# Distance penalty moved into a per-head mask tile, and the 64-row second pass paired on two row halves

## The chip, the cores and the metric

The kernel runs on one core of a Trainium2 chip. The metric is the time of one execution on the device in microseconds; three runs of the kernel before the change are given. The profile is one further, profiled execution of the same program.

## The reference

One layer of a decoder block on 512 tokens of width 1024: RMSNorm, one wide input projection, two token mixers side by side (gated linear attention, GLA, and sparse attention, NSA), a merge, an output projection, and a SwiGLU feed-forward part. The change touches NSA alone. It has 8 heads of width 64 in 2 groups, and three branches; the selected branch ("s") and the window branch ("w") both come to a causal attention over 512 keys, each with its own keys and values, because 8 blocks of 64 keys exist and up to 16 are selected, and the window is 512 wide. What both compute:

```
slopes = exp2(-8 * (h + 1) / 8)                     # 2^-(h+1), h = 0..7
s = q @ k.T - slopes * (t - pos)                    # distance penalty
s = where(pos <= t, s, -1e30)
p = softmax(s);  o = p @ v
out = gate0 * o_compressed + gate1 * o_selected + gate2 * o_window
```

## The kernel before

**Numbers.** All data is four-byte. A product is split into high and low parts (`whi`, `wlo`; `hT_hi`, `hT_lo`), and three matmuls (hi·hi, lo·hi, hi·lo; lines 182 to 184) make one k-step of a dense product.

**The stages** run in this order: token-wise projections, GLA beside further projections, compression for NSA, the attention loop, the merge and output projection, the feed-forward part. The program is written for a scheduler: the order in the code, with the readiness of data, sets the order on each engine; pools of buffers with a fixed number of turns (`bufs`) set when a buffer comes free. PSUM banks are taken by tag, two to a tag: `sc` for scores, `tp` for transposes, `acc` for a head's output, `mm` for dense products.

**The attention loop** (`attention`, line 846) runs over 16 units: head h = 0 to 7, and for each head the branches s and w. In a unit it turns the probabilities of this unit by TensorE transposes (L792), splits them into `ph` (ScalarE, L199) and `pl` (VectorE, L200), and multiplies them with the values (L806, L807, L809). Between these it does the scores of the unit two ahead, and fills gaps with single k-steps of dense products (`fill`, lines 182 to 184), eight k-steps a unit, which is one dense product. The weights of these are converted by ScalarE (L59 `whi`, L62 `wlo`) and finished by an accumulating DMA that GpSimd issues (L63 `wlo`), one in most units.

**Scores** (`scores`, line 727). The 512 queries are four blocks of 128; block i needs 128 (i + 1) keys, so its products have 128, 256, 384 or 512 columns. A unit's four blocks go in three parts: block 3 in one PSUM bank; blocks 0 and 2 in another; block 1 in a third turn. The first pass (L742) multiplies `q1`, which holds the high part of the query on one half of the 128 rows and its low part on the other, with `ka`, which holds the high part of the keys on both halves. The second pass (L743) multiplies `q3`, the high query on rows 0 to 63 and two more rows, with `kb`, the low part of the keys on rows 0 to 63 and two more rows. The two extra rows (64 and 65, from `augq` and `augk`) carry the distance penalty: -slope · t times 1, and slope times pos. Hence 66 rows. VectorE then adds the causal mask, negates and takes the row's extreme in one operation (L750, `causal` is 128 x 512 with zeros and a triangle of -1e30 at its right end), and ScalarE exponentiates (L752).

`head_setup` (line 710) makes `q1` and `q3` of a head, once per head, two heads ahead; `group_keys` (line 696) makes `ka` and `kb` once per group and branch.

**Elsewhere, for reference:** L632 and L638 are two small products of the compression, on rows 0 to 63 and on rows 64 to 127; L183 behind L638 is a part of a dense product.

Of the kernel before, what the change touches and what calls it, by code (L numbers as in the profile page):

```python
# [8 lines left out]
F32 = mybir.dt.float32  # L9
F32R = mybir.dt.float32r  # L10
U8 = mybir.dt.uint8
AF = mybir.ActivationFunctionType
OP = mybir.AluOpType
# [3 lines left out]
S = 512  # L17
# [8 lines left out]
NEG = -1e30  # L26
# [66 lines left out]
def hybrid_block_kernel(ctx: ExitStack, tc: tile.TileContext, I, outT):  # L93
    nc = tc.nc
    act, dve, pool, pe = nc.scalar, nc.vector, nc.gpsimd, nc.tensor
# [5 lines left out]
    def bank(tag):  # L101
        return psum.tile([128, 512], F32, tag=tag, bufs=2, name="ps_" + tag)
# [52 lines left out]
    for key in with_gla + with_cmp + with_att + late:  # L155
        kind, n = key
# [45 lines left out]
    def token_sums(acc, tag, blocks=range(NT)):  # L202

        ps = bank(tag)
        for a in range(len(acc)):
            for i in blocks:
                pe.matmul(ps[:, i:i + 1], acc[a][:, i * 128:(i + 1) * 128], ones[:, 0:1],
                          start=(a == 0 and i == blocks[0]), stop=(a == len(acc) - 1), skip_group_check=True)
        return ps
# [6 lines left out]
    def over_partitions(rs, tag, blocks=range(NT), after=None):  # L216
        ps = bank(tag)
        with tc.issue_after(after.ins) if after else nullcontext():
            for i in blocks:
                pe.matmul(ps[:, i * 128:(i + 1) * 128], rs[:, i:i + 1].to_broadcast([128, 128]), ident,  # L220
                          start=True, stop=True)
        return ps
# [6 lines left out]
    for k in range(KD):  # L229
        xt = xin.tile([128, S], F32, tag="xt", bufs=8, name="xt")  # L230
        nc.sync.dma_start(xt, I["xT"][k])
        if k % 2 == 0:
            st.ahead_to(min(k // 2 + 1, 2))
        last = act.activation(out=hT[:, k, :], in_=xt, func=AF.Copy, scale=g_pre[:, k:k + 1])
        dve.scalar_tensor_tensor(out=hTl[:, k, :], in0=xt, scalar=g_pre[:, k:k + 1],
                                 in1=hT[:, k, :].bitcast(F32), op0=OP.mult, op1=OP.subtract)
# [12 lines left out]
    for g in range(3):  # L249
        pss = [bank(t) for t in tags[g]]  # L250
        for c in range(4):
            wh, wl = st.next(("tok", g, c))
            for i in range(NT):
                if (g, c, i) == (0, 3, 2):
                    ps = token_sums([acc_x], "acc")
                    rsqrt_mean(rs_x, ps[:, 0:NT], D, EPS)
                t = slice(i * 128, (i + 1) * 128)
                for kk in range(2):
                    k = 2 * c + kk
                    w = slice(kk * TG, (kk + 1) * TG)  # L260
                    o = pss[i][:, 0:TG]
# [3 lines left out]
        if g == 0:  # L265
            ps = over_partitions(rs_x, "acc")
            act.copy(rb_x, ps)
            p_in.__exit__(None, None, None)
            mid = p_mid.__enter__()
# [5 lines left out]
        for i in range(NT):  # L275
            c0, c1 = g * TG, (g + 1) * TG
            if c0 < 1024:
                act.activation(out=tok[i][:, c0:min(c1, 1024)], in_=pss[i][:, 0:min(c1, 1024) - c0], func=AF.Copy,
                               scale=rs_x[:, i:i + 1])
            if c1 > 1024:  # L280
                act.activation(out=tokb[:, i, 0:c1 - 1024], in_=pss[i][:, 1024 - c0:TG], func=AF.Copy,
                               scale=rs_x[:, i:i + 1])
    C_VS, C_VW, C_GATE, C_A = 0, 128, 256, 280

    causal = mid.tile([128, S], F32, name="causal")
    pool.memset(causal, 0.0)
    pool.dma_start(causal[:, S - 128:S], I["tril_neg"])
    qst = [mid.tile([128, S], F32, tag="qst%d" % i, name="qst%d" % i) for i in range(4)]
    kst = {b: mid.tile([128, S], F32, name="kst" + b) for b in "sw"}
    gq = [base.tile([128, S], F32, tag="b%d" % h, name="gq%d" % h) for h in range(HG)]  # L290
# [26 lines left out]
    for i in range(2):  # L317
        t = gt.tile([128, NT, 128], F32, name="at%d" % i)
# [233 lines left out]
    mid2 = p_mid2.__enter__()  # L552
    p_nsa = tc.tile_pool(name="nsa", bufs=1, reuse_waits="tile")
    nsa = p_nsa.__enter__()
    augq = nsa.tile([66, S], F32, name="augq")
    pool.dma_start(augq[64:66], I["aug"][:, 0, :])
    gates = nsa.tile([128, NT, 24], F32, name="gates")
    act.activation(out=gates, in_=tokb[:, :, C_GATE:C_GATE + 24], func=AF.Tanh, scale=0.5)
    dve.tensor_scalar(out=gates, in0=gates, scalar1=0.5, scalar2=0.5, op0=OP.mult, op1=OP.add)
# [9 lines left out]
    p_sco = tc.tile_pool(name="sco", bufs=1, reuse_waits="tile", side="right")  # L569
    cmp = p_cmp.__enter__()  # L570
    cin = p_cin.__enter__()
    augk = cin.tile([66, S], F32, name="augk")
    pool.dma_start(augk[64:66], I["aug"][:, 1, :])
    cmp_bias = cmp.tile([128, NT, HN, 32], F32, name="cmp_bias")
    pool.dma_start(cmp_bias, I["cmp_bias"])
    cmp_mask = cmp.tile([128, NT, 32], F32, name="cmp_mask")
# [112 lines left out]
    ka, kb, vv = {}, {}, {}  # L689
    for b in "sw":  # L690
        kb[b] = nsa.tile([128, S], F32R, name="kb" + b)
        ka[b] = nsa.tile([128, S], F32R, name="ka" + b)
        vv[b] = nsa.tile([128, NT, 128], F32R, name="vv" + b)
        pool.tensor_copy(kb[b][64:66, :], augk[64:66, :])

    def group_keys(g, b):
        a, o = slice(g * 64, g * 64 + 64), slice((1 - g) * 64, (1 - g) * 64 + 64)
        act.copy(ka[b][a, :], kst[b][a, :])
        dve.tensor_copy(ka[b][o, :], kst[b][a, :])
        dve.tensor_tensor(out=kb[b][0:64, :], in0=kst[b][a, :], in1=ka[b][a, :].bitcast(F32), op=OP.subtract)  # L700

    def group_values(g, b):
        c = (C_VS if b == "s" else C_VW) + g * 64
# [4 lines left out]
    heads = {}  # L708

    def head_setup(h):  # L710
        e = h % 2
        q = qst[h // 2]
        a, o = slice(e * 64, e * 64 + 64), slice((1 - e) * 64, (1 - e) * 64 + 64)
        q1 = nsa.tile([128, S], F32R, tag="q1", bufs=2, name="q1")
        q3 = nsa.tile([66, S], F32R, tag="q3", bufs=2, name="q3")
        act.copy(q1[a, :], q[a, :])
        dve.tensor_tensor(out=q1[o, :], in0=q[a, :], in1=q1[a, :].bitcast(F32), op=OP.subtract)
        act.copy(q3[0:64, :], q[a, :])
        dve.tensor_scalar(out=q3[64:66, :], in0=augq[64:66, :], scalar1=2.0 ** -(h + 1), scalar2=None,
                           op0=OP.mult)  # L720
        heads[h] = (q1, q3)

    OFF = [0, 128, 384, 768]
    sco = []
# [1 line left out]

    def scores(h, b):

        q1, q3 = heads[h]
        p = sco[0].tile([128, 1280], F32, tag="p", bufs=3, name="p")  # L730
        mx = sco[0].tile([128, NT], F32, tag="mx", bufs=3, name="mx")
        z = sco[0].tile([128, NT], F32, tag="z", bufs=3, name="z")
        units[h, b] = p

        def part(blks, last):
            ps = bank("sc")
            col = 0
            for i in blks:
                n = 128 * (i + 1)
                s = ps[:, col:col + n]  # L740
                t = slice(i * 128, (i + 1) * 128)
                pe.matmul(s, q1[:, t], ka[b][:, 0:n], start=True, stop=False)  # L742
                pe.matmul(s, q3[0:66, t], kb[b][0:66, 0:n], start=False, stop=True)  # L743
                col += n
            col = 0
            for i in blks:
                n = 128 * (i + 1)
                s = ps[:, col:col + n]
                o = p[:, OFF[i]:OFF[i] + n]
                dve.tensor_tensor_reduce(out=o, in0=s, in1=causal[:, S - n:S], scale=-1.0, scalar=-NEG,  # L750
                                         op0=OP.add, op1=OP.min, accum_out=mx[:, i:i + 1])
                act.activation(out=o, in_=o, func=AF.Exp, scale=-1.0, bias=mx[:, i:i + 1],  # L752
                               accum_out=z[:, i:i + 1])
                col += n
            if last:
                dve.reciprocal(z, z)
                dve.tensor_tensor(out=z, in0=z, in1=gates[:, :, 3 * h + (1 if b == "s" else 2)], op=OP.mult)
                for i in range(NT):
                    n = 128 * (i + 1)
                    o = p[:, OFF[i]:OFF[i] + n]  # L760
                    dve.tensor_scalar(out=o, in0=o, scalar1=z[:, i:i + 1], scalar2=None, op0=OP.mult)

        return [lambda: part((3,), False), lambda: part((0, 2), False), lambda: part((1,), True)]

    accs = {}

# [60 lines left out]
    def begin(u):  # L827
        h, b = u
        if h % 4 == 0:
            group_keys(h // 4, b)  # L830
        return scores(h, b)

    def first_scores():

        parts = []

        def start():
            p_cin.__exit__(None, None, None)
            sco.append(p_sco.__enter__())
            head_setup(0)  # L840
            for u in order_u[:2]:
                parts.extend(begin(u))

        return [start] + [lambda i=i: parts[i]() for i in range(6)] + [lambda: head_setup(1)]

    def attention(fill):

        head_compressed(0)
        for i, (h, b) in enumerate(order_u):
            nxt = begin(order_u[i + 2]) if i + 2 < len(order_u) else [lambda: None] * 3  # L850
            if b == "s":
                head_start(h)
            elif h + 2 < HN:
                head_setup(h + 2)
# [34 lines left out]
    q = Pieces(with_att)  # L889
# [8 lines left out]
    for n in range(8):  # L898
        ps = bank("sc")
# [60 lines left out]
    for n in range(3):  # L960
        ps = bank("mm")
# [120 lines left out]
    made = {}  # L1082
# [199 lines left out]
    first = (bank("sc"), bank("sc"))  # L1282
# [23 lines left out]
    third = (bank("acc"), bank("acc"))  # L1306
# [22 lines left out]
    for n in range(N0, KF):  # L1329
# [3 lines left out]
        last = unit(n, rest_of_forms if n == N0 else None)  # L1333
# [98 lines left out]
    for n in range(8):  # L1432
        ps = bank("acc" if n % 2 == 0 else "tp")
# [195 lines left out]
```

## Time and profile before

| | |
|---|---|
| time, median of 3 runs | 872.35 us (871.92 to 873.64) |
| profiled execution, span of its instructions | 870.5 us, 13817 instructions |
| profiled execution, its own time | not recorded beside its span; the runs' median lies 1.9 us above the span |
| TensorE busy | 856.8 us (98%), 5268 matmuls |
| TensorE weight loads | 759.8 us (87%) |
| VectorE, ScalarE, GpSimd busy | 594.5 (68%), 486.3 (56%), 141.5 us (16%) |

How to read it: PE is TensorE's matmuls, PEld its weight loads (shown apart, since a load runs under the matmul before it), DVE is VectorE, ACT ScalarE, POOL GpSimd. L742 is line 742 of the kernel. A matmul's shown duration contains its way through the array, so a row of matmuls overlaps; the distance from one start to the next is what it costs. Form 64\*128 means 64 rows and 128 columns of the array in use.

### The profile page before, as it was taken

What the parts mean: (1) busy time and instruction counts of PE and PEld (TensorE: products, weight loads), DVE (VectorE), ACT (ScalarE), POOL (GpSimd) and SP (SyncE); (2) the same over time, 40 slices, a digit from 0 to 9 for tenths busy, and PEclk for the clock granted to TensorE, in tenths of its full rate; (3) what the DMA queues carried; (4) which work ended last, traced back from release to release, by engine and by line L of the source; (5) the groups of instructions that cost most, each with busy time, mean ns of one, the idle gap of its engine ahead of it and who ended that gap; (6) DMA issues with size and microseconds to landing.
All of it is one profiled execution on the core that took longest, in us unless ns stands there. A gap on an engine that the chain in (4) does not pass through costs nothing.

```text
span 870.5 us, 13817 instructions
## 1 busy us (share of the span) xinstructions
PE 856.8 (98%) x5268; PEld 759.8 (87%) x5268; DVE 594.5 (68%) x1125; ACT 486.3 (56%) x862; POOL 141.5 (16%) x169
## 2 busy tenths in 40 slices
PE   9999999999999999999999999999999999999995
PEld 8998877887888788888887999899999999889995
DVE  8224753534464888887767468998778779829876
ACT  7335434333362788888744577765666656525441
POOL 1000322020030001000000354111111110001343
PEclk9999999999999999999999999999999999999998
DMA  7332221222241444545317849679877873335222
GB/s 237 97 98 93 97 83 63 79 66 74 73 152 49 120 98 103 117 98 122 85 49 226 269 137 247 125 199 233 186 171 176 195 176 85 94 87 170 86 98 98
DMA packets 36914, 111.23 MB, mean 128 GB/s; under 512 B 4236, under 2 KB 6300, under 8 KB 36720
## 3 DMA queue, kind: packets, MB, share of 16 engines
q1 hardware_dynamic: 27232, 82.49, 29.7%
q0 software_dynamic: 8896, 27.32, 16.8%
q8 instruction: 41, 0.67, 0.3%
q10 hardware_dynamic: 720, 0.54, 0.2%
q14 instruction: 25, 0.20, 0.1%
HBM read 95.66 MB, written 4.19 MB: 115 GB/s over the span
## 4 chain that ended last, share of the span: by engine, by line
PE 91%; ACT 4%; DVE 2%; issue 1%; DMA 1%; POOL 0%; SPq 0%; ACTq 0%; DVEq 0%; POOLq 0%
PE ps_mm L182 11%; PE ps_mm L184 11%; PE ps_mm L183 11%; PE ps_mm L1191 6%; PE ps_tp L1191 6%; PE ps_sc L1191 5%; PE ps_acc L1191 5%; PE ps_sc L1482 4%; PE ps_acc L1482 2%; PE ps_mm L1482 2%; PE ps_tp L792 2%; PE ps_acc L184 1%; PE ps_acc L183 1%; PE ps_acc L182 1%; PE ps_sc L182 1%; PE ps_sc L184 1%
## 5 line engine op out<-in xcount | busy, mean ns | idle before, releaser
L59 ACT CAST whi<-wraw 128x1024 fp32r<-128x1024 f32 (+2 forms) x81 | 80.1, 989 | 150.4 <-PE ps_mm L183 66.9
L182 PE MATMUL ps_mm<-hT_hi,whi 128*128 128x512 f32 x344 | 139.9, 407 | 0.0
L184 PE MATMUL ps_mm<-hT_hi,wlo 128*128 128x512 f32 x344 | 137.0, 398 | 0.0
L183 PE MATMUL ps_mm<-hT_lo,whi 128*128 128x512 f32 x344 | 136.1, 395 | 0.0
L65 DVE TENSOR_TENSOR wlo<-wraw,whi 128x1024 fp32r<-128x1024 f32 (+2 forms) x66 | 75.0, 1137 | 51.1 <-ACT whi L59 51.0
L184 PEld LDWEIGHTS ps_mm<-hT_hi,wlo 128*128 128x128 f32 x344 | 64.7, 188 | 15.4 <-DVE wlo L65 0.3
L182 PEld LDWEIGHTS ps_mm<-hT_hi,whi 128*128 128x128 f32 x344 | 64.9, 189 | 14.0
L183 PEld LDWEIGHTS ps_mm<-hT_lo,whi 128*128 128x128 f32 x344 | 64.9, 189 | 13.0
L752 ACT ACTIVATE p<-p,mx 128x512 f32<-128x512 f32 (+1 forms) x64 | 35.9, 561 | 8.8 <-DVE mx L750 7.8
L200 DVE TENSOR_TENSOR pl<-ps_tp,ph 128x512 fp32r<-128x512 f32 (+1 forms) x64 | 31.0, 489 | 13.2 <-ACT ph L199 12.5
L63 POOL DMA_DIRECT2D wlo<-wraw x15 | 13.0, 864 | 154.2 <-ACT wlo L62 154.2
L750 DVE CUSTOM_DVE_ANT_0 p<-ps_sc,causal 128x512 f32<-128x512 f32 (+1 forms) x64 | 30.2, 486 | 6.2 <-PE ps_sc L743 6.1
L1090 POOL DMA_DIRECT2D w_uu<-in_w_up x19 | 16.4, 865 | 84.6 <-PE ps_sc L1191 27.0
L199 ACT CAST ph<-ps_tp 128x512 fp32r<-128x512 f32 (+1 forms) x64 | 26.3, 415 | 4.1 <-PE ps_tp L792 3.6
L792 PE MATMUL ps_tp<-ident,p 128*128 128x128 f32 x160 | 27.7, 273 | 0.4 <-ACT pc L686 0.3
L792 PEld LDWEIGHTS ps_tp<-ident,p 128*128 128x128 f32 x160 | 20.6, 140 | 8.0 <-ACT pc L686 0.7
L182 PE MATMUL ps_mm<-gla_hi,whi 128*128 128x512 f32 x64 | 26.2, 410 | 0.0
L466 DVE TENSOR_TENSOR sr<-ps_mm,rb_x 128x512 f32<-128x512 f32 x8 | 5.5, 692 | 29.0 <-PE ps_mm L184 29.0
L184 PE MATMUL ps_mm<-gla_hi,wlo 128*128 128x512 f32 x64 | 25.3, 395 | 0.0
L183 PE MATMUL ps_mm<-gla_lo,whi 128*128 128x512 f32 x64 | 25.3, 395 | 0.0
L1106 ACT CAST w_hl<-s 128x1024 fp32r<-128x1024 f32 x12 | 12.6, 1047 | 19.6 <-issue 15.8
L1106 ACT CAST w_d1h<-s 128x1024 fp32r<-128x1024 f32 x13 | 13.7, 1051 | 17.2 <-issue 12.5
(862 smaller groups left out, 2778.2 us busy)
## 6 DMA issues: line engine op xcount, KB each, us to landing
wraw<-in_w_t SPq DMA_DIRECT2D x40, 512.0 KB, 3.5
wraw<-in_w_gate SPq DMA_DIRECT2D x21, 512.0 KB, 5.8
rw<-in_w_up SPq DMA_DIRECT2D x19, 512.0 KB, 4.2
wlo<-wraw POOLq DMA_DIRECT2D x15, 512.0 KB, 4.5
wlo<-in_w_gate POOLq DMA_DIRECT2D x13, 512.0 KB, 7.2
wraw<-in_w_tok SPq DMA_DIRECT2D x12, 440.0 KB, 4.1
w_uu<-in_w_up POOLq DMA_DIRECT2D x19, 256.0 KB, 5.8
wraw<-in_w_proj SPq DMA_DIRECT2D x8, 512.0 KB, 3.5
```

The source lines that it names most:

```text
L59: self.nc.scalar.copy(hi[:, :cols], raw[:, :cols])
L65: self.nc.vector.tensor_tensor(out=lo[:, :cols], in0=raw[:, :cols], in1=hi[:, :cols].bitcast(F32), op=OP.subtract)
L182: pe.matmul(ps[:, t], wh[:, c], xh(k)[:, t], start=(k == 0), stop=False)
L183: pe.matmul(ps[:, t], wh[:, c], xl(k)[:, t], start=False, stop=False)
L184: marks.append(pe.matmul(ps[:, t], wl[:, c], xh(k)[:, t], start=False, stop=(k == ktot - 1)))
L199: act.copy(hi, src)
L200: dve.tensor_tensor(out=lo, in0=src, in1=hi.bitcast(F32), op=OP.subtract)
L750: dve.tensor_tensor_reduce(out=o, in0=s, in1=causal[:, S - n:S], scale=-1.0, scalar=-NEG, op0=OP.add, op1=OP.min, accum_out=mx[:, i:i + 1])
L752: act.activation(out=o, in_=o, func=AF.Exp, scale=-1.0, bias=mx[:, i:i + 1], accum_out=z[:, i:i + 1])
L792: pe.transpose(tp[:, i * 128:(i + 1) * 128], p[:, OFF[i] + k * 128:OFF[i] + (k + 1) * 128], ident)
L1191: pe.matmul(o, w[:, c], x[q], start=(first and q == 0 and i == 0), stop=(q == 3 and i == 2), skip_group_check=True)
L1482: pe.matmul(o, w[:, c], x[q], start=(first and q == 0 and i == 0), stop=(q == KH - 1 and i == 2), skip_group_check=True)
```

## The change

A tile of 128 x 512 per head takes the place of `causal`: it holds the distance penalty and the causal mask together, and VectorE's operation reads it instead (L760 after). Two such tiles take turns (`alibi`). GpSimd makes them: a DMA broadcasts the positions, a second one adds the triangle, the first operation adds -t per row and halves, and each later head's tile is half of the one before. The mask value is halved with it and stays far below every score. The two extra rows, `augq`, `augk` and their copies go, and the second pass has 64 rows.

```diff
-    causal = mid.tile([128, S], F32, name="causal")
-    pool.memset(causal, 0.0)
-    pool.dma_start(causal[:, S - 128:S], I["tril_neg"])
+    alibi = [mid.tile([128, S], F32, name="alibi%d" % i) for i in range(2)]
+    pool.dma_start(alibi[0], I["aug"][1, 1, :].partition_broadcast(128))
+    pool.dma_start(alibi[0][:, S - 128:S], I["tril_neg"], accum_op=OP.add)
+    alibi_row = mid.tile([128, 1], F32, name="alibi_row")
+    pool.dma_start(alibi_row, I["aug"][0, 0, S - 128:S].unsqueeze(1))
...
-    augq = nsa.tile([66, S], F32, name="augq")
-    pool.dma_start(augq[64:66], I["aug"][:, 0, :])
...
-        pool.tensor_copy(kb[b][64:66, :], augk[64:66, :])
...
-        dve.tensor_tensor(out=kb[b][0:64, :], in0=kst[b][a, :], in1=ka[b][a, :].bitcast(F32), op=OP.subtract)
+        for r in (a, o):
+            dve.tensor_tensor(out=kb[b][r, :], in0=kst[b][a, :], in1=ka[b][a, :].bitcast(F32), op=OP.subtract)
...
-        q3 = nsa.tile([66, S], F32R, tag="q3", bufs=2, name="q3")
+        q2 = nsa.tile([128, S], F32R, tag="q2", bufs=2, name="q2")
+        cb = alibi[(h + 1) % 2]
...
-        act.copy(q3[0:64, :], q[a, :])
-        dve.tensor_scalar(out=q3[64:66, :], in0=augq[64:66, :], scalar1=2.0 ** -(h + 1), scalar2=None,
-                           op0=OP.mult)
-        heads[h] = (q1, q3)
+        act.copy(q2[o, :], q[a, :])
+        if h == 0:
+            pool.tensor_scalar(out=cb, in0=alibi[0], scalar1=alibi_row, scalar2=0.5, op0=OP.add, op1=OP.mult)
+        else:
+            pool.tensor_scalar(out=cb, in0=alibi[h % 2], scalar1=0.5, scalar2=None, op0=OP.mult)
+        heads[h] = (q1, (q1, q2) if e == 0 else (q2, q1), cb)
...
+        def products(groups):
+            banks = [bank("sc") for _ in groups]
+            for ps, blks in zip(banks, groups):
+                for i, n, c in cols(blks):
+                    pe.matmul(ps[:, c], q1[:, i * 128:(i + 1) * 128], ka[b][:, 0:n], start=(i == blks[0]),
+                              stop=False, skip_group_check=True)
+            for e, (ps, blks) in enumerate(zip(banks, groups)):
+                for i, n, c in cols(blks):
+                    pe.matmul(ps[:, c], his[e][half[e], i * 128:(i + 1) * 128], kb[b][half[e], 0:n],
+                              start=False, stop=True, skip_group_check=True)
+            return banks
...
+        def first():
+            made.extend(products(((3,), (0, 2))))
+            softmax(made[0], (3,), False)
+
+        def third():
+            softmax(products(((1,),))[0], (1,), True)
+
+        return [first, lambda: softmax(made[1], (0, 2), False), third]
```

The high query now stands on both row halves, in `q1` on one and in `q2` on the other, and the low keys on both halves of `kb`. Block 3's second pass runs on rows 0 to 63 and those of blocks 0 and 2 on rows 64 to 127, into another bank; block 1's runs on rows 0 to 63 alone. The matmuls are as many as before.

On TensorE, a unit's scores stood in two places, with two k-steps and transposes between them (`ps_sc` are scores, `ps_tp` transposes, `ps_mm` dense products). Before:

```order
L792 MATMUL ps_tp<-ident,p 128x128 x4
L742 MATMUL ps_sc<-kaw,q_2308 128x512
L743 MATMUL ps_sc<-kbw,q_2309 128x512
L182 MATMUL ps_mm<-gla_hi,whi 128x512
L183 MATMUL ps_mm<-gla_lo,whi 128x512
L184 MATMUL ps_mm<-gla_hi,wlo 128x512
L182 MATMUL ps_mm<-gla_hi,whi 128x512
L183 MATMUL ps_mm<-gla_lo,whi 128x512
L184 MATMUL ps_mm<-gla_hi,wlo 128x512
L792 MATMUL ps_tp<-ident,p 128x128 x3
L742 MATMUL ps_sc<-kaw,q_2308 128x128
L743 MATMUL ps_sc<-kbw,q_2309 128x128
```

The same unit after (L748 is the first pass, L752 the second, L810 the transposes; `q_2307` is `q1`, `q_2308` is `q2`):

```order
L810 MATMUL ps_tp<-ident,p 128x128 x4
L748 MATMUL ps_sc<-kaw,q_2307 128x512
L748 MATMUL ps_sc<-kaw,q_2307 128x128
L748 MATMUL ps_sc<-kaw,q_2307 128x384
L752 MATMUL ps_sc<-kbw,q_2308 128x512
L752 MATMUL ps_sc<-kbw,q_2307 128x128
L752 MATMUL ps_sc<-kbw,q_2307 128x384
L182 MATMUL ps_mm<-gla_hi,whi 128x512
L183 MATMUL ps_mm<-gla_lo,whi 128x512
L184 MATMUL ps_mm<-gla_hi,wlo 128x512
```

First and second passes of blocks 3, 0 and 2 now stand together ahead of the two k-steps, the three first passes first; the part of blocks 0 and 2 moved up by two k-steps and the second transposes. Block 1's part stays behind the third transposes.

On GpSimd, the pieces around the start of the attention loop (`wlo` are the accumulating DMAs of the dense weights). Before:

```order
L694 CAST kbs<-augk 2x512
L694 CAST kbw<-augk 2x512
L594 COPY ct<-cpe 128x16 x2
L63 DMA wlo<-wraw 128x1024 x15
L955 TENSOR_TENSOR acc_4264<-acc_4264,nsq 128x512 x2
```

After:

```order
L592 COPY ct<-cpe 128x16 x2
L63 DMA wlo<-wraw 128x1024
L721 TENSOR_SCALAR alibi_574<-alibi_573 128x512
L63 DMA wlo<-wraw 128x1024 x2
L721 TENSOR_SCALAR alibi_573<-alibi_574 128x512
L63 DMA wlo<-wraw 128x1024 x2
```

The two casts are gone, and six halvings stand among the fifteen issues, one per head from head 2 on. The tiles of heads 0 and 1 are made early, behind the DMAs of `alibi`, ahead of GLA's first work on GpSimd.

On VectorE, the same unit as above for TensorE (`pl` is the remainder of transposed probabilities, the ISA rows are the mask operation and its row extreme `mx`). Before:

```order
L750 ISA p,mx<-ps_sc,causal 128x512
L750 ISA mx 128x1
L200 TENSOR_TENSOR pl<-ps_tp,ph 128x512
L200 TENSOR_TENSOR pl<-ps_tp,ph 128x384
L750 ISA p,mx<-ps_sc,causal 128x128
L750 ISA mx 128x1
L750 ISA p,mx<-ps_sc,causal 128x384
```

After:

```order
L760 ISA p,mx<-ps_sc,alibi_573 128x512
L760 ISA mx 128x1
L200 TENSOR_TENSOR pl<-ps_tp,ph 128x512
L760 ISA p,mx<-ps_sc,alibi_573 128x128
L760 ISA mx 128x1
L760 ISA p,mx<-ps_sc,alibi_573 128x384
L760 ISA mx 128x1
L200 TENSOR_TENSOR pl<-ps_tp,ph 128x384
```

The operations on blocks 0 and 2 moved ahead of the second transposes' remainder.

More of the change, by code (lines that the diff above doesn't have):

```diff
@@ L571, in hybrid_block_kernel @@
     cin = p_cin.__enter__()
-    augk = cin.tile([66, S], F32, name="augk")
-    pool.dma_start(augk[64:66], I["aug"][:, 1, :])
     cmp_bias = cmp.tile([128, NT, HN, 32], F32, name="cmp_bias")
@@ L727, in scores @@
     def scores(h, b):
-        q1, q3 = heads[h]
+        q1, his, cb = heads[h]
         p = sco[0].tile([128, 1280], F32, tag="p", bufs=3, name="p")
@@ L733, in scores, with cols, softmax @@
         units[h, b] = p
-        def part(blks, last):
-            ps = bank("sc")
-            col = 0
+        half = (slice(0, 64), slice(64, 128))
+        def cols(blks):
+            at, col = [], 0
             for i in blks:
[L739 to L748, printed above, removed]
+                at.append((i, 128 * (i + 1), slice(col, col + 128 * (i + 1))))
+                col += 128 * (i + 1)
+            return at
+        def products(groups):
[9 more added lines that the diff above has]
+            return banks
+        def softmax(ps, blks, last):
+            for i, n, c in cols(blks):
+                s = ps[:, c]
                 o = p[:, OFF[i]:OFF[i] + n]
-                dve.tensor_tensor_reduce(out=o, in0=s, in1=causal[:, S - n:S], scale=-1.0, scalar=-NEG,
+                dve.tensor_tensor_reduce(out=o, in0=s, in1=cb[:, S - n:S], scale=-1.0, scalar=-NEG,
                                          op0=OP.add, op1=OP.min, accum_out=mx[:, i:i + 1])
@@ L753, in part @@
                                accum_out=z[:, i:i + 1])
-                col += n
             if last:
@@ L761, in part @@
                     dve.tensor_scalar(out=o, in0=o, scalar1=z[:, i:i + 1], scalar2=None, op0=OP.mult)
-        return [lambda: part((3,), False), lambda: part((0, 2), False), lambda: part((1,), True)]
+        made = []
+        def first():
[4 more added lines that the diff above has]
+        return [first, lambda: softmax(made[1], (0, 2), False), third]
     accs = {}
```

## The prediction

> **What bounds the kernel now.** I read the page's span, its busy line and its chain first, then the attention stage alone, because every line that the change touches works there or feeds it.
>
> ```profile
> span 870.5 us, 13817 instructions
> PE 856.8 (98%) x5268; PEld 759.8 (87%) x5268; DVE 594.5 (68%) x1125; ACT 486.3 (56%) x862; POOL 141.5 (16%) x169
> PE 91%; ACT 4%; DVE 2%; issue 1%; DMA 1%; POOL 0%; SPq 0%; ACTq 0%; DVEq 0%; POOLq 0%
> 298.00:438.00 140.00, 139.32 (x752) 113.97 (x750) 113.27 (x326) 116.18 (x259) 11.16 (x13) 1.00 0.45 105
> ```
>
> The last row is the attention loop, from its first transposes to its end: us, then busy PE, PEld, DVE, ACT and POOL, then the granted clock (1.00). TensorE is never idle for long, VectorE and ScalarE are busy 81% and 83% of the time. The waits of the same stretch say whether TensorE waits for them:
>
> ```profile
> POOL wlo L63 <- ACT wlo L62: 114.1, 13, 11.4
> ...
> PEld ps_acc L807 <- DVE pl L200: 2.3, 6, 0.5
> ...
> PEld ps_tp L792 <- ACT pc L686: 0.7, 1, 0.7
> PEld ps_tp L792 <- DVE pl L200: 0.6, 1, 0.6
> ```
>
> Columns: total us, times, longest. TensorE's weight loads wait under 4 us in 140, and part of that lies under a running matmul. So a microsecond added to TensorE's own work here is a microsecond of the end, and one taken away is gained until ScalarE, 17% behind, ends last. The chain of waits gives the price of each matmul as the distance to the next. One unit (a head and a branch; there are 16):
>
> ```profile
> 326.12 0.44 PE ps_tp L792 x4
> 326.56 0.23 PE ps_sc L742
> 326.79 0.23 PE ps_sc L743
> ...
> 328.74 0.06 PE ps_sc L742
> 328.80 0.11 PE ps_sc L743
> 328.92 0.22 PE ps_sc L742
> 329.14 0.18 PE ps_sc L743
> ...
> 330.69 0.12 PE ps_sc L742
> 330.81 0.12 PE ps_sc L743
> ...
> 335.56 0.44 PE ps_tp L792 x4
> ```
>
> A unit is 335.56 - 326.12 = 9.4 us. The L742 and L743 rows are block 3 (512 columns), blocks 0 and 2 (128 and 384), block 1 (256). A second pass (L743) costs 0.23 + 0.11 + 0.18 + 0.12 = 0.64 us a unit, 10.2 us in all. From 256 to 512 columns is 0.11 us, so 0.43 ns a column: 512 columns stream in 0.22 us, and about 0.01 is lost between matmuls. The 128 columns cost 0.11, not 0.06, and the weight loads say why:
>
> ```profile
> 328.58 0.19 PEld L743 LDWEIGHTS ps_sc<-kbw,q 66*128 66x128 f32 x1
> 328.69 0.19 PEld L742 LDWEIGHTS ps_sc<-kaw,q 128*128 128x128 f32 x1
> 328.81 0.19 PEld L743 LDWEIGHTS ps_sc<-kbw,q 66*128 66x128 f32 x1
> ```
>
> A load occupies its path for 0.11 us, with 66 rows as with 128, and normally lies under the matmul before it.
>
> **The change, part by part.**
>
> *The pair.* Block 3's second pass (0.23) now stands beside those of blocks 0 and 2 (0.11 + 0.18), on the other 64 rows: 0.52 us a unit is at stake. Nothing in the trace runs two matmuls at once. Bounds: no overlap, gain 0; whole overlap, 0.23 remains and the gain is 0.29. Three loads are still needed, and the rows show them one after the other: with block 0's load at the start of block 3's matmul, the other half ends 0.11 + 0.11 + 0.16 (384 columns) = 0.38 later, 0.39 with the gap. I take that, since its 0.11 is a row: 0.13 gained a unit, 2.1 us in 16. Block 1's pass has no partner and gains nothing.
>
> *The switches.* Before, 66 rows use the whole array; now 64 rows use half, so each unit goes from the whole array to halves and back twice (pair, block 1): 4 x 16 = 64 switches. Nearly no row of before shows one, but the compression does: L638 multiplies on rows 64 to 127, and the next instruction is a whole-array matmul (L183), which waits for no semaphore.
>
> ```profile
> 273.78 0.19 PEld L638 LDWEIGHTS ps_sc<-cw,chid 64*64 64x64 f32 x2
> 274.03 0.19 PEld L183 LDWEIGHTS ps_mm<-hT_lo,whi 128*128 128x128 f32 x1
> 274.14 0.19 PEld L184 LDWEIGHTS ps_mm<-hT_hi,wlo 128*128 128x128 f32 x1
> ```
> ```profile
> 273.78 0.32 PE L638 MATMUL ps_sc<-cw,chid 64*64 64x64 f32 x2
> 274.04 0.50 PE L183 MATMUL ps_mm<-hT_lo,whi 128*128 128x512 f32 x1
> ```
> ```profile
> L638 PE MATMUL ps_sc<-cw,chid x2: 218/242/267, 273.8 to 273.9; 64*64 64x64 f32 x2
> ```
>
> L638's second matmul takes 0.22, so it started at 273.78 + 0.32 - 0.22 = 273.88. The next load should start then; it starts 0.15 later. 64 columns stream in 0.03, so 0.12 us pass until the array is empty, and then the load itself is uncovered (the load behind it, L184's, starts another 0.11 later, when L183's own matmul can start). That this is no matter of columns or of a narrow matmul is shown by L807, which uses 64 columns and all rows:
>
> ```profile
> 332.73 0.28 PE L807 MATMUL ps_acc<-pl,vvw 128*64 128x256 f32 x1
> ```
> ```profile
> 332.73 0.19 PEld L182 LDWEIGHTS ps_mm<-gla_hi,whi 128*128 128x128 f32 x1
> ```
>
> There the whole-array load starts with the matmul, at 332.73: no wait. So a switch of rows costs 0.12 (emptying) + 0.11 (uncovered load) - about 0.02 of gaps = 0.21 us behind a matmul of 256 or more columns. Bounds: 0 (if L638 is a special case) and 0.23. At L638 itself, where 0.11 of load was the pace anyway, it was 0.14. I take 0.21, because that is what these rows give for long matmuls: 64 x 0.21 = 13.4 us.
>
> The Trainium skill, "TensorEngine Tiling (Array Packing)", Key Properties, says that changing the tiling mode, not just the tile, drains TensorE. The L638 rows agree (0.12 us), the L807 rows show no such drain for a change of columns alone; by the page each of the 64 switches drains, and its sum is the one above.
>
> *VectorE and ScalarE.* The rows of augq go, and each group's key remainder is written on both halves:
>
> ```profile
> L719 DVE TENSOR_SCALAR q<-augq 2x512 fp32r<-2x512 f32 x8 | 3.3, 418 | 0.2
> L700 DVE TENSOR_TENSOR kbs<-ksts,kas 64x512 fp32r<-64x512 f32 x2 | 1.7, 872 | 0.1
> L700 DVE TENSOR_TENSOR kbw<-kstw,kaw 64x512 fp32r<-64x512 f32 x2 | 1.4, 684 | 0.0
> ```
>
> Minus 8 x 0.42 = 3.3, plus 4 x 0.69 to 0.87 = 3.1: nothing, and TensorE covers it. The mask operand of the reduction keeps its shape; ScalarE's second copy only changes its rows. VectorE now gets three reductions together ahead of the remainder of the second transposes; it has 19% to spare, and if it has not, L807 waits, at most 0.5 us at a time as above.
>
> *GpSimd.* At the start one memset and one DMA become three DMAs and two operations, each behind the last one's landing. They stand where GpSimd has nothing to do:
>
> ```profile
> 25.77 0.60 POOL L287 DMA_DIRECT2D causal<-in_tril_neg  x1
> 95.05 0.73 POOL L391 TENSOR_TENSOR gke<-gk,e 128x256 f32<-128x256 f32 x1 [68.68 <-ACT el L375]
> ```
> ```profile
> DMA to landing us min/median/max: 2.2/2.2/2.2
> ```
>
> The last row is L287's DMA. 68 us cover three such landings and two operations, some 10 us. Two DMAs of augq and augk and two casts go. Six halvings of 128x512 stand among the issues of wlo; each has a unit (9.4 us) before its head needs it. Bounds for one: a memset of that shape and a two-operand sum.
>
> ```profile
> L319 POOL MEMSET at<- 128x512 f32 x2 | 1.1, 549 | 0.0
> L1503 POOL TENSOR_TENSOR acc<-acc,nsq 128x512 f32<-128x512 f32 x3 | 6.8, 2272 | 20.8 <-ACT nsq L1502 10.8 <-ACT acc L1499 10.0
> ```
>
> 0.55 to 2.3 us; I take 1.1 (one operand, nearer the memset). The 114 us in which GpSimd waits for ScalarE cover six of them. They wait for reductions that ended over a unit earlier, so the DMAs behind them are not held up. Cost nothing.
>
> **Sum.** 13.4 - 2.1 = 11.3 us more for TensorE. A later TensorE waits less for VectorE: of the listed waits I let 1 us vanish. So +10.3: a span of 870.5 + 10.3 = 880.8 us. The runs' median, 872.35, lies 1.9 above the profiled span; added to it, 882.7. I say 882.
>
> **The rivals.**
> 1. *Both kinds of switch cost, as summed* (0.48). With a pair that overlaps wholly and switches at 0.14 it is 9.0 - 4.6 - 1 = +3.4; with no overlap and nothing absorbed +13.4. So 875.8 to 885.8 at its ends, mostly 878 to 885.
> 2. *Only the way back costs* (0.16): the half-array load may slip under a running whole-array matmul; L638 shows a way back only. 32 x 0.21 - 2.1 - 0.5 = +4.1: 876.5.
> 3. *Switches are free and the pair overlaps* (0.26), the case on the other side. Place: the second pass of blocks 0, 2 and 3. Price: 16 x 0.13 to 0.29 = 2.1 to 4.6 us gained, 867.8 to 870.3. For it speaks that L638 is one event, a four-byte product with an own wait ahead of it; against it that L183 waits for nothing else. It decides where a switch costs under 0.13 / 4 = 0.03 us (0.07 with whole overlap).
> 4. *No overlap and no switch cost* (0.10): the change does not do what it says, the halves run one after the other: within 1 us, 872.4.
>
> The Trainium skill, "TensorE: Matmul & The Clock Gate", Part 3, says that matmuls on different row groups run at once, a few ns apart. By it the pair costs 0.23; no run here shows it; with free switches that is rival 3's lower end, 867.8.
>
> **How the numbers follow.** About 0.2% (1.7 us) is what a measurement of this kernel can tell from no change. Rivals 1 and 2 are slower (0.64), 4 is the same (0.10), 3 is faster (0.26). The likeliest gives 882; its own range is 878 to 885. The range for 8 in 10 must reach rivals 2 and 4 and half of 3: 869 to 884.5 leaves out 0.13 of rival 3 below and some 0.05 of rival 1 above.
>
> **What would show it.** Right: in the profile after, the load behind a second-pass matmul starts 0.1 us or more after that matmul would have streamed, TensorE's attention stage grows by some 10 us with as many instructions, and VectorE and ScalarE wait more for it. Pair: blocks 0 and 2 start while block 3 streams. Wrong: loads of the half-array products start together with the matmul before them, as L182's does behind L807; then rival 3 or 4. GpSimd wrong: reductions that wait for the penalty tile.

## The result, and the profile after

| | before | after |
|---|---|---|
| time, median (all runs of this comparison) | 872.13 us (871.91 to 873.64) | 883.59 us (883.39 to 884.14) |
| span of the profiled execution | 870.5 us | 881.6 us |

The ratio is 1.0131 (95% interval 1.0118 to 1.0144): the change costs 11.5 us. It lies inside the predicted range (869 to 884.5), 1.6 us above the predicted time. In the comparisons below, one run of the kernel before and the profiled run of `pinned` came at a granted clock of 0.675 and 0.655, took over 1150 us and are left out of every time, so `pinned` has no row for stage and idle time.

The page of after, span, busy times and chain, and then the window of the attention stage (columns as above: us, then busy PE, PEld, DVE, ACT, POOL, clock):

```profile
span 881.6 us, 13830 instructions
PE 866.2 (98%) x5268; PEld 758.7 (86%) x5268; DVE 593.8 (67%) x1121; ACT 488.4 (55%) x862; POOL 151.7 (17%) x174
PE 89%; ACT 5%; DVE 3%; issue 1%; DMA 1%; POOL 0%; SPq 0%; POOLq 0%; ACTq 0%; DVEq 0%
298.00:448.00 150.00, 148.57 (x756) 114.44 (x755) 112.82 (x323) 117.94 (x259) 21.59 (x20) 1.00 0.41 99
```

As many matmuls as before, and 9.4 us more of TensorE's busy time; VectorE and ScalarE have nearly the same work (593.8 for 594.5 us, 488.4 for 486.3). On the chain, TensorE's share falls from 91 to 89% while ScalarE's and VectorE's rise by one each: some waits for them are new. Where the time went is told by the first start of the first pass (L742, L748 after) and the last start of L806 (L824 after), a product with `ph`, from the instruction lists of the two kernels:

```profile
L742 PE MATMUL ps_sc<-kas,q x32: 218/376/481, 281.3 to 415.6; 128*128 128x512 f32 x8, 128*128 128x128 f32 x8, 128*128 128x384 f32 x8, 128*128 128x256 f32 x8
...
L806 PE MATMUL ps_acc<-ph,vvw x24: 280/336/497, 310.5 to 440.4; 128*128 128x512 f32 x8, 128*128 128x384 f32 x8, 128*128 128x256 f32 x8
```
```profile
L748 PE MATMUL ps_sc<-kas,q x32: 221/374/478, 282.0 to 424.9; 128*128 128x512 f32 x8, 128*128 128x128 f32 x8, 128*128 128x384 f32 x8, 128*128 128x256 f32 x8
...
L824 PE MATMUL ps_acc<-ph,vvw x24: 277/439/497, 312.7 to 451.4; 128*128 128x512 f32 x8, 128*128 128x384 f32 x8, 128*128 128x256 f32 x8
```

The stage takes 440.4 - 281.3 = 159.1 us before and 451.4 - 282.0 = 169.4 after: 10.3 of the 11.1 us by which the span grew. "Stage" below means this distance.

The unit that the prediction took apart, in the chain of after:

```profile
330.20 0.52 PE ps_sc L748 x3
330.71 0.48 PE ps_sc L752 x2
331.19 0.43 PE ps_mm L182
331.62 0.23 PE ps_mm L183
...
334.50 0.12 PE ps_sc L748
334.62 0.31 PE ps_sc L752
334.93 0.37 PE ps_acc L824
335.30 0.18 PE ps_acc L825
```

Block 1's second pass costs 0.31 where it cost 0.12, and the product behind it (384 columns) 0.37 where the next of the same width costs 0.18: two switches of 0.19. The three second passes of blocks 3, 0 and 2 cost 0.48 instead of 0.23 + 0.11 + 0.18 = 0.52, and the dense product behind them 0.43 where the next costs 0.23. Together 0.55 us a unit: 0.38 at block 1, 0.16 at the pair. In 16 units that is 8.8 us. If the pair's entrance costs 0.19 too (same_half below bears it out), 0.29 of its 0.48 us are left for the products, and that is 0.11 + 0.18 of blocks 0 and 2 alone: block 3's 0.23 is hidden whole.

The weight loads of the pair, and behind it the whole array again; in square brackets the idle time ahead and what ended it:

```profile
329.93 0.53 PEld L748 LDWEIGHTS ps_sc<-kaw,q 128*128 128x128 f32 x3
330.64 0.30 PEld L752 LDWEIGHTS ps_sc<-kbw,q 64*128 64x128 f32 x3 [0.18 <-issue]
331.12 0.19 PEld L182 LDWEIGHTS ps_mm<-gla_hi,whi 128*128 128x128 f32 x1 [0.18 <-issue]
331.23 0.19 PEld L183 LDWEIGHTS ps_mm<-gla_lo,whi 128*128 128x128 f32 x1
```

Both directions wait 0.18 us, for nothing that the profile names (`issue`). L183's load follows L182's at the usual 0.11. And the halves run at once: in a window from 330.643 to 330.70 stand two loads and two matmuls, of block 3 and of block 0.

```profile
330.64 0.19 PEld L752 LDWEIGHTS ps_sc<-kbw,q 64*128 64x128 f32 x2 [0.18 <-issue]
...
330.64 0.50 PE L752 MATMUL ps_sc<-kbw,q 64*128 64x512 f32 x2
```

Two loads of 0.18 us each take 0.19 together.

The 8.8 us leave 1.5 of the 10.3 to waits of TensorE. Its longest in the attention stage, switches among them (columns: total us, times, longest):

```profile
PEld ps_acc L825 <- DVE pl L200: 3.4, 8, 0.5
PEld ps_mm L182 <- issue: 2.6, 14, 0.2
PEld ps_sc L752 <- issue: 2.6, 14, 0.2
...
PEld ps_acc L824 <- ACT ph L199: 1.5, 5, 0.4
```

The two `issue` rows are the pair's switches. The `pl` row was 2.3 us before (as L807), and the `ph` row is new at this size (0.3 before, as L806). What makes it was not in the prediction; the experiments find it.

### The profile page after: what moved, and what is told of

It is laid out like the page before. It is cut to its first block, busy times and chain, and to the rows that moved or that the text cites. A ratio compares the mean times of both kernels' runs of the same rounds, so it can differ in the third digit from the quotient of the medians.

```text
span 881.6 us, 13830 instructions
## 1 busy us (share of the span) xinstructions
PE 866.2 (98%) x5268; PEld 758.7 (86%) x5268; DVE 593.8 (67%) x1121; ACT 488.4 (55%) x862; POOL 151.7 (17%) x174
## 4 chain that ended last, share of the span: by engine, by line
PE 89%; ACT 5%; DVE 3%; issue 1%; DMA 1%; POOL 0%; SPq 0%; POOLq 0%; ACTq 0%; DVEq 0%
PE ps_mm L182 10%; PE ps_mm L184 10%; PE ps_mm L183 10%; PE ps_mm L1209 6%; PE ps_tp L1209 5%; PE ps_sc L1209 5%; PE ps_acc L1209 5%; PE ps_sc L1500 4%; PE ps_acc L1500 2%; PE ps_mm L1500 2%; PE ps_acc L182 1%; PE ps_acc L184 1%; PE ps_acc L183 1%; PE ps_tp L810 1%; PE ps_sc L182 1%; PE ps_sc L183 1%
## 5 line engine op out<-in xcount | busy, mean ns | idle before, releaser
L182 PE MATMUL ps_mm<-hT_hi,whi 128*128 128x512 f32 x344 | 140.9, 410 | 0.0
L183 PE MATMUL ps_mm<-hT_lo,whi 128*128 128x512 f32 x344 | 136.0, 395 | 0.0
L182 PEld LDWEIGHTS ps_mm<-hT_hi,whi 128*128 128x128 f32 x344 | 64.7, 188 | 15.6 <-issue 1.5
L183 PEld LDWEIGHTS ps_mm<-hT_lo,whi 128*128 128x128 f32 x344 | 64.8, 188 | 12.7
L760 DVE CUSTOM_DVE_ANT_0 p<-ps_sc,alibi 128x512 f32<-128x512 f32 (+1 forms) x64 | 29.8, 486 | 13.0 <-PE ps_sc L752 12.6
L810 PE MATMUL ps_tp<-ident,p 128*128 128x128 f32 x160 | 27.7, 272 | 0.0
L810 PEld LDWEIGHTS ps_tp<-ident,p 128*128 128x128 f32 x160 | 20.9, 140 | 7.2
L182 PE MATMUL ps_mm<-gla_hi,whi 128*128 128x512 f32 x64 | 26.9, 421 | 0.0
L183 PE MATMUL ps_mm<-gla_lo,whi 128*128 128x512 f32 x64 | 25.3, 395 | 0.0
```

Source lines behind the costliest of these rows:

```text
L182: pe.matmul(ps[:, t], wh[:, c], xh(k)[:, t], start=(k == 0), stop=False)
L183: pe.matmul(ps[:, t], wh[:, c], xl(k)[:, t], start=False, stop=False)
L760: dve.tensor_tensor_reduce(out=o, in0=s, in1=cb[:, S - n:S], scale=-1.0, scalar=-NEG, op0=OP.add, op1=OP.min, accum_out=mx[:, i:i + 1])
L810: pe.transpose(tp[:, i * 128:(i + 1) * 128], p[:, OFF[i] + k * 128:OFF[i] + (k + 1) * 128], ident)
```

## The experiments

The theory ahead of them: the switches are the cost, and the pair gives part of it back. The rival: something else in the change (the mask tile, the copies, the order) costs a share. "Whole array" means the second pass on all 128 rows with the whole of `q1`, high query on one half and low on the other, against the low keys on both halves. That adds the product of the two low parts to the scores and needs no switch. All variants were timed beside the kernel before, whose median was 872.9 us beside whole_array, pair_only, single_only and same_half, and 872.8 beside the other four. TensorE's idle time is 150 us less its busy time in that window; a matmul's shown duration covers a part of each wait, so it shows less than was lost.

| kernel | time (us) | ratio to before, interval | stage (us) | TensorE idle in 298 to 448 (us) |
|---|---|---|---|---|
| before | 872.1 | | 159.1 | 0.7 |
| after | 883.6 | 1.0131 (1.0118 to 1.0144) | 169.4 | 1.4 |
| whole_array | 878.9 | 1.0065 (1.0048 to 1.0081) | 163.5 | 3.7 |
| pair_only | 881.0 | 1.0089 (1.0074 to 1.0105) | 165.7 | 2.8 |
| single_only | 881.0 | 1.0093 (1.0078 to 1.0108) | 167.0 | 2.3 |
| same_half | 885.8 | 1.0147 (1.0130 to 1.0165) | 171.3 | 0.3 |
| whole_old_order | 874.4 | 1.0019 (1.0009 to 1.0029) | 159.8 | 1.2 |
| before_moved | 878.7 | 1.0063 (1.0047 to 1.0080) | 164.1 | 3.7 |
| before_64rows | 893.9 | 1.0239 (1.0224 to 1.0254) | 180.2 | 0.0 |
| pinned | 881.6 | 1.0103 (1.0086 to 1.0120) | | |

**whole_array: no switches at all.** After, with all second passes on the whole array; mask tile, copies and order stay.

```diff
-                    pe.matmul(ps[:, c], his[e][half[e], i * 128:(i + 1) * 128], kb[b][half[e], 0:n],
+                    pe.matmul(ps[:, c], q1[:, i * 128:(i + 1) * 128], kb[b][:, 0:n],
```

> The changed kernel with all second passes on the whole array: 128 rows, q1 against kb (the low-by-low product comes in as well, on rows that the halves leave out). Mask tile, order and the copy q2 stay. Theory (64 switches at 0.19 us, pair gains 0.23 us a unit): 883.6 - 64 x 0.19 + 16 x 0.23 = 875 us; 872 if the 2.4 us of further waits go with the switches. Rival (mask tile, GpSimd and the moved blocks cost it): about 883.

878.93 us. So taking every switch out gives back only 4.7 of the 11.5 us (875 was expected), and 6 us of cost stand in a kernel that has none. The waits of TensorE, from 298 to 445 us:

```profile
PEld ps_acc L825 <- DVE pl L200: 3.6, 7, 0.9
PEld ps_acc L824 <- ACT ph L199: 3.3, 6, 0.8
...
PE ps_acc L824 <- ACT ph L199: 2.0, 5, 0.6
```

TensorE now waits for `ph`, ScalarE's part of the split of the transposed probabilities, which it hardly did before (0.3 us in the same window).

**pair_only and single_only: one kind of switch each.** pair_only takes block 1 back to the whole array, single_only takes the pair (blocks 3, 0, 2) back:

```diff
 # pair_only; single_only has "if i != 1"
+                    if i == 1:
+                        pe.matmul(ps[:, c], q1[:, i * 128:(i + 1) * 128], kb[b][:, 0:n],
+                                  start=False, stop=True, skip_group_check=True)
+                    else:
                         pe.matmul(ps[:, c], his[e][half[e], i * 128:(i + 1) * 128], kb[b][half[e], 0:n],
...
```

> Block 1's second pass on the whole array (q1 against kb), the pair stays on halves: 32 switches fewer, overlap kept. Theory: 883.6 - 32 x 0.19 = 877.5 us. Rival (order and mask tile): 883. Rival (the way back into the whole array alone costs): the same 877.5, with the load ahead of the pair starting at the matmul before it.

> Blocks 3, 0 and 2 on the whole array (q1 against kb), block 1 stays on 64 rows: 32 switches fewer, overlap lost. Theory: 883.6 - 6.1 + 3.6 = 881 us. Rival (the pair does not overlap): 877.5. Rival (order and mask tile): 883.

880.97 and 881.00 us. With the pair on the whole array (single_only) 2.6 us are gained, which is the 16 x 0.16 of the chain. Without block 1's switches (pair_only) it should have been 16 x 0.38 = 6.1, and it is 2.6 too; the expected 877.5 was missed by 3.5. TensorE's idle time in the window doubles instead, from 1.4 to 2.8 us, and its weight loads wait 2.6 us for `ph` where they waited 1.5. Block 1's switches stand directly ahead of the product that waits for `ph` (L824): TensorE spends there in switching what it would otherwise spend in waiting. The rows of one unit that show it stand further down, under "The costs do not add".

**same_half: the pair without its overlap.** All second passes on rows 0 to 63.

```diff
-                    pe.matmul(ps[:, c], his[e][half[e], i * 128:(i + 1) * 128], kb[b][half[e], 0:n],
+                    pe.matmul(ps[:, c], his[0][half[0], i * 128:(i + 1) * 128], kb[b][half[0], 0:n],
```

> All second passes on rows 0 to 63: as many switches, no two halves at once. Theory: the pair's overlap of 0.23 us a unit is lost, 883.6 + 3.6 = 887 us. Rival (no overlap in the changed kernel either): 883.6.

885.82 us, 2.2 more than after. In its weight loads the three second passes, one behind the other, hold the array from 331.28 to 331.99, 0.71 us to the next whole-array load; in after it is 330.64 to 331.12, 0.48:

```profile
331.28 0.53 PEld L752 LDWEIGHTS ps_sc<-kbw,q 64*128 64x128 f32 x3 [0.18 <-issue]
331.99 0.19 PEld L182 LDWEIGHTS ps_mm<-gla_hi,whi 128*128 128x128 f32 x1 [0.18 <-issue]
```

The overlap is worth 0.23 us a unit, 3.7 in 16. That only 2.2 reach the end fits its TensorE, which is idle 0.3 instead of 1.4 us in the window. The switches are the same two with one half in use: 0.71 less the 0.52 that the three passes took before is 0.19 for the entrance.

**before_moved: the order alone.** Before, with the first and second passes of blocks 0 and 2 issued behind those of block 3, as in after, and nothing else: same 66 rows, same mask, no switch.

```diff
...
-        return [lambda: part((3,), False), lambda: part((0, 2), False), lambda: part((1,), True)]
+        made = []
+
+        def first():
+            made.extend([products((3,)), products((0, 2))])
+            part(made[0], (3,), False)
+
+        return [first, lambda: part(made[1], (0, 2), False), lambda: part(products((1,)), (1,), True)]
```

> The kernel before with nothing but the order changed: both passes of blocks 0 and 2 stand behind those of block 3, ahead of the dense k-steps. 66 rows, no mask tile. Theory A: 872.5 + 6 = 878.5 us. Theory B: 872.5.

878.69 us: 5.9 slower than before (4.1 to 7.0), by the order alone, and as slow as whole_array. Five of them are in the stage (164.1 against 159.1). TensorE's list of waits there has no row for a PSUM bank, so the two banks that are now taken together cost nothing that is seen. ScalarE in one unit of branch s, for before and for before_moved (L752 and L755 are the exponentials, L773 and L782 a cast for the compressed branch):

```profile
376.35 0.71 ACT L752 ACTIVATE p<-p,mx 128x512 f32<-128x512 f32 x1
376.96 0.19 ACT L752 ACTIVATION_READ_ACCUMULATOR p<-p,mx 128x1 f32 x1
377.05 0.47 ACT L199 CAST ph<-ps_tp 128x384 fp32r<-128x384 f32 x1
377.54 0.62 ACT L773 CAST c<-pc 32x512 fp32r<-32x512 f32 x1
378.19 0.40 ACT L752 ACTIVATE p<-p,mx 128x128 f32<-128x128 f32 x1
```
```profile
380.21 0.71 ACT L755 ACTIVATE p<-p,mx 128x512 f32<-128x512 f32 x1
380.83 0.19 ACT L755 ACTIVATION_READ_ACCUMULATOR p<-p,mx 128x1 f32 x1
380.92 0.39 ACT L755 ACTIVATE p<-p,mx 128x128 f32<-128x128 f32 x1
381.21 0.19 ACT L755 ACTIVATION_READ_ACCUMULATOR p<-p,mx 128x1 f32 x1
381.41 0.62 ACT L782 CAST c<-pc 32x512 fp32r<-32x512 f32 x1
382.05 0.48 ACT L199 CAST ph<-ps_tp 128x384 fp32r<-128x384 f32 x1
```

Before, the `ph` of the second transposes follows the 512-column exponential at once. With the scores of block 0 there earlier, its exponential and the cast come first, and `ph` is 1.13 us later in the row (382.05 - 380.92). The weight loads of before_moved show who pays, with L743 as block 1's second pass, L815 the product with `ph`, L816 that with `pl`:

```profile
381.83 0.19 PEld L743 LDWEIGHTS ps_sc<-kbs,q 66*128 66x128 f32 x1
382.58 0.19 PEld L815 LDWEIGHTS ps_acc<-ph,vvs 128*128 128x128 f32 x1 [0.56 <-ACT ph L199]
383.18 0.13 PEld L816 LDWEIGHTS ps_acc<-pl,vvs 128*64 128x64 f32 x1 [0.41 <-DVE pl L200]
```

First `ph`, then `pl`, which VectorE can only make from it: near one microsecond without a load in this unit. Of the seven times that weight loads wait for `ph` in the stage (3.8 us together), six stand in units of branch s, where casts for the compressed branch stand in the row too, and one in the last unit; in the other units of branch w, block 0's exponential alone makes no such wait. The window of the same kernel has ScalarE busy for 118.88 of 150 us, 79%, no more than before (120.45):

```profile
298.00:448.00 150.00, 146.29 (x776) 118.12 (x774) 115.17 (x331) 118.88 (x265) 12.04 (x14) 1.00 0.44 102
```

It is late by its order, not by its load.

**whole_old_order: the mask tile alone.** Whole array, no second query copy, and blocks 0 and 2 back behind the second transposes.

```diff
...
         def first():
-            made.extend(products(((3,), (0, 2))))
-            softmax(made[0], (3,), False)
+            softmax(products(((3,),))[0], (3,), False)
+
+        def second():
+            softmax(products(((0, 2),))[0], (0, 2), False)
...
```

> Mask tile as in the changed kernel, second pass on the whole array (q1 against kb, no q2 copy), and blocks 0 and 2 back behind the second transposes. Theory A (moving blocks 0 and 2 up costs some 6 us, since their exponentials then stand ahead of ph of the second transposes on ScalarE): 871 to 873 us. Theory B (the mask tile or GpSimd costs it): as whole_array, 879.

874.36 us, 1.6 above the kernel before beside it (0.8 to 2.5 by the interval of the ratio, 1.0009 to 1.0029). So much is the price of the mask tile, its GpSimd work and the second half of the low keys together, 0.7 of it in the stage; what makes the rest was not pursued. Going from this kernel to whole_array adds the order and one query copy, and 4.6 us.

**before_64rows: the switch alone, eight in a unit.** Before, with 64 rows in the second pass. It leaves out the two rows of the distance penalty, so it computes the scores without it.

```diff
-                pe.matmul(s, q3[0:66, t], kb[b][0:66, 0:n], start=False, stop=True)
+                pe.matmul(s, q3[0:64, t], kb[b][0:64, 0:n], start=False, stop=True)
```

> The kernel before with the second pass on 64 rows: it leaves out the two rows of the distance penalty. First and second pass alternate, so 8 switches a unit, 128 in all, and no halves at once. Switches of 0.19 us: 872.5 + 24 = 897 us, less what ScalarE's waits take up. If only the way back costs: 884.5.

893.86 us, 21.1 above before, and the stage is 180.2 - 159.1 = 21.1 longer. That is 21.1 / 128 = 0.165 us a switch, with two rows of multiplication fewer and no other change. The chain of one unit (blocks 0 and 2, whose rows were 0.06, 0.11, 0.22 and 0.18 before) shows the single prices:

```profile
335.25 0.06 PE ps_sc L742
335.32 0.26 PE ps_sc L743
335.57 0.37 PE ps_sc L742
335.94 0.37 PE ps_sc L743
```

In and out of block 0's 128 columns a switch costs 0.15, into block 2's 384 it costs 0.19. The other five of this unit cost 0.19 or 0.20, so the eight come to 1.48 us, 23.7 in 16 units. That 2.6 of these do not reach the end fits waits that are used up: TensorE has no idle time left in the window (0.7 us before).

**pinned: after, with the order on VectorE and ScalarE put back.** The products stay paired ahead of the second transposes, but VectorE's operation on blocks 0 and 2 is held behind the `pl` of the second transposes, and the exponentials with it.

```diff
...
-                dve.tensor_tensor_reduce(out=o, in0=s, in1=cb[:, S - n:S], scale=-1.0, scalar=-NEG,
-                                         op0=OP.add, op1=OP.min, accum_out=mx[:, i:i + 1])
+                with tc.issue_after(after.ins) if after else nullcontext():
+                    dve.tensor_tensor_reduce(out=o, in0=s, in1=cb[:, S - n:S], scale=-1.0, scalar=-NEG,
+                                             op0=OP.add, op1=OP.min, accum_out=mx[:, i:i + 1])
...
```

> The changed kernel with its halves and its product order, but VectorE's operations on blocks 0 and 2 held behind pl of the second transposes, as they stood before. Theory A, with the halves' own price of 0.55 us a unit read from the profile after: 872.4 + 8.8 = 881 us, 2.5 less than the changed kernel. If the two costs simply add: 883.6 - 6 = 877.6. Theory B: 883.6.

881.6 us (881.19 to 883.29, three runs). That is 8.8 us above its own before, just what the chain of after gives for switches and pair, and 2.7 us less than the 11.5 of after, though the two intervals just touch (up to 1.0120, from 1.0118 on), so the 2.7 are likely rather than shown. The order on ScalarE in its trace is as meant: `ph` of the second transposes comes ahead of block 0's exponential. No version beat the kernel before.

## Why the prediction was right, and which of its steps were not

**The switches: right.** 64 of them, both ways, at 0.19 us each in the chain where 0.21 was taken from L638: 12.2 us for 13.4. before_64rows shows the switch alone, at 0.15 to 0.20 in its chain and 0.165 in its time. The load behind a half-array matmul starts late, as the prediction said it would show. A change of columns alone still costs nothing: in after, L825's matmul and the whole-array load behind it start together.

```profile
333.19 0.19 PEld L182 LDWEIGHTS ps_mm<-gla_hi,whi 128*128 128x128 f32 x1
...
333.19 0.39 PE L825 MATMUL ps_acc<-pl,vvw 128*64 128x512 f32 x1
```

**The pair: right in kind, too small.** 0.23 us a unit against 0.13, 3.7 against 2.1 us. The step that failed is "three loads are still needed, and the rows show them one after the other": the first two run at once, and only block 2's follows 0.11 later. The Trainium skill, "TensorEngine Tiling (Array Packing)", Key Properties, says that different tiles can load weights and multiply in parallel; the two loads in 0.19 us agree.

**Rivals.** 2 (only the way back costs) and 3 (switches free) fall with the two rows of 0.18 and with before_64rows, 4 (no overlap, no switch cost) with same_half as well.

**A later TensorE waits less, minus 1 us: wrong in sign.** Switches less overlap are 8.5 us by these terms, 8.8 by the chain; measured are 11.5. The prediction named the place (VectorE gets three reductions ahead of the remainder, and L807 waits) and priced it at nothing, because VectorE "has 19% to spare". The runs show an order that costs 5.9 us when nothing else is changed. Here the busy share said nothing on when one result comes; and it was ScalarE, which that step left out, that came late first.

**The costs do not add.** The prediction's first step, that a microsecond added to TensorE's work is one of the end, holds only where TensorE would not wait. 5.9 for the order and 8.8 for the switches would be 14.7 us above before. In after it is 11.5: block 1's switches stand where TensorE would wait anyway. The unit shown above for before_moved, in after:

```profile
384.94 0.18 PEld L752 LDWEIGHTS ps_sc<-kbs,q 64*128 64x128 f32 x1
385.32 0.19 PEld L824 LDWEIGHTS ps_acc<-ph,vvs 128*128 128x128 f32 x1 [0.20 <-ACT ph L199]
385.92 0.13 PEld L825 LDWEIGHTS ps_acc<-pl,vvs 128*64 128x64 f32 x1 [0.41 <-DVE pl L200]
```

The wait for `ph` is 0.20 where it was 0.56, and the 0.36 between them are about the two switches (0.38). So the order adds some 2.7 us net, by pinned and by subtraction of the chain's 8.8 alike; 1.5 of it are seen in the stage (10.3 - 8.8). Another 0.7 lies ahead of the stage (its start, 281.3 and 282.0), where the profiles of these kernels differ by up to 1.7 us (before_moved starts at 283.0); no run explains that part.

**That the sum came out near was partly luck.** Two errors oppose each other: a net cost of switches and pair 2.5 us under the forecast's 11.3, and 2.7 us of order where 1 less was allowed for. The sum itself gave 882.7, and 882 was said.

**GpSimd: no cost, as said, but a step wrong.** Halvings take 1.48 us where 1.1 was taken, and the list of this operation names nobody who waits for it. But they did not find their reductions ended "over a unit earlier": six of them waited 24.2 us for these in the stage, 6.1 at the longest. No wait of TensorE for a weight DMA is in its list, so this cost nothing that is seen.

```profile
L721 POOL TENSOR_SCALAR alibi<-alibi x7: 1482/1484/1907, 31.3 to 396.1; 128x512 f32<-128x512 f32 x7
```
```profile
POOL alibi L721 <- DVE mx L760: 24.2, 6, 6.1
```

## What to carry to other kernels

Packing small products on row halves had an entrance and an exit here, 0.19 us each, and would pay only if more than 0.38 us ran doubled between them. At the 0.43 ns a column of these rows that is an estimate of some 900 columns on each half, where this kernel had 512; a single half-array product between whole-array ones, like block 1's, gained nothing for its 0.38. When a block of work is moved up on the bounding engine, write down for every in-order engine behind it what now stands ahead of the result that the bounding engine needs next, whatever share of its time is free.

## What the hardware showed that was not expected

- Two weight loads of different row halves run at once: 0.19 us for two of 0.18, where whole-array loads follow at 0.11.
- The switch costs the same on the way in as on the way back (0.19 us each at block 1, 0.18 of idle loads each at the pair). No load of a half slipped under a whole-array matmul here, as rival 2 had supposed it might.
- A switch is cheaper at a short matmul: 0.15 us at the 128-column passes of before_64rows, 0.19 or 0.20 at its longer ones. At 128 columns a load was the pace already (0.11 us a matmul before, not 0.06), and that this is the reason is argued, not shown.
